# The first norm of a decoder block from tokens laid out by channels, with a product with ones in place of transposes

## The chip, the core and the metric

The kernel runs on one core of one Trainium2 chip. The metric is device time in microseconds (us); lower is better. Five engines work side by side, each through its own queue in a fixed order: TensorE (PE in the profile; PEld is its weight load), VectorE (DVE), ScalarE (ACT), GpSimd (POOL) and SyncE (SP), which here only issues DMAs. Every engine waits at the head of its own queue, so an instruction that waits holds up all that stand behind it on that engine.

## The reference

One decoder block over 2048 tokens of 1024 channels, in float32. What matters here is its beginning:

```
h    = x * rsqrt(mean(x*x, over channels) + 1e-6) * norm_pre_mix
proj = h @ w_in                       # 1024 -> 5376
q, k = rope(proj[:, :768]), rope(proj[:, 768:1536])
v    = proj[:, 1536:2304]             # 12 heads x 64
u, z, gate_a, gate_b = ...            # the remaining columns
```

Behind it follow dilated window attention, a gated branch, an output product, a second norm and an MLP. The norm's factor is one number per token, so it may stand ahead of a product with `h` or, for the rows that the product gives, behind it.

## The kernel before

Products in near-float32 accuracy are made of three: each operand is split into a high part (rounded to fp32r) and the rest, and `mm3` (lines 95 to 97) issues high by high, high by rest and rest by high. So every operand costs an ACT copy (high) and a DVE subtraction (rest).

The tokens are worked in four chunks `c` of 512 tokens, each of four blocks `i` of 128; block (0, 2) is the third of the first chunk. The tile `hT_a` holds a chunk of `h` with channels on the partitions, eight groups `k` of 128 channels, as high and rest. The program's start, up to about 87 us, runs `v_block` for the chunks 0 and 1: for a block, 24 matmuls 128x512 into the PSUM tile `va` (two of the three column groups of v), then 24 matmuls 128x256 into `vb`. In `v_block`, after the fourth of the eight `k` of `va`, a callback `between` puts the next block's `prenorm_cols` into PE's order. So the next block of `hT_a` has to be ready when the 12 remaining matmuls of `va` and the 24 of `vb` are done. Behind the v blocks come the q and k products of chunks 0 and 1 (`qk_pair`), and in the last of these pairs the four blocks of chunk 2 are normed; then v of chunks 2 and 3 (about 221 to 292 us), where `between` norms chunk 3.

Before the change a block's norm has two steps. `prenorm_rows` works with tokens on the partitions, one number per token: ACT squares with a running sum (line 204, two halves), DVE adds the halves and makes the reciprocal root in `rstd_of` (128x1 tensors, with one Newton step), and one DVE instruction scales the block in place (line 208). It is issued a block ahead. `prenorm_cols` then has PE transpose the eight 128x128 squares into two PSUM banks `pt` (line 219); ACT copies each bank into the high part (line 222), DVE subtracts for the rest (line 223), ACT copies once more into `hr` (line 245), which goes to memory (`hTd`). Block (0, 0) does the same with its gain broadcast through a product (`gpre`).

PE's order is the order in which the code is written. ACT, DVE, POOL and SP are ordered by a scheduler, except for the piece `as_written` at the start, which loads and splits the first v weights (`raw`, `wv`).

Of the kernel before, what the change touches and what calls it, by code (L numbers as in the profile page):

```python
# [41 lines left out]
def block_kernel(ctx, tc, a, out):  # L42
# [56 lines left out]
    def rstd_of(pl, ss, n, scale, tag):  # L99

        r = pl.tile([P, n], F32, name=f"r_{tag}", tag=f"rs_r{n}")
        act.activation(r, ss, AF.Sqrt, bias=eps, scale=scale)  # L102
        v = pl.tile([P, n], F32, name=f"v_{tag}", tag=f"rs_v{n}")
        dve.tensor_scalar(v, ss, scale, EPS, op0=OP.mult, op1=OP.add)
        dve.reciprocal(r, r)  # L105
        t = pl.tile([P, n], F32, name=f"t_{tag}", tag=f"rs_t{n}")
        if n == 1:
            dve.scalar_tensor_tensor(t, r, v, r, op0=OP.mult, op1=OP.mult)  # L108
        else:
            dve.tensor_mul(t, r, r)  # L110
            dve.tensor_mul(t, t, v)
        dve.tensor_scalar(t, t, -0.5, 1.5, op0=OP.mult, op1=OP.add)  # L112
        dve.tensor_mul(r, r, t)  # L113
        return r
# [60 lines left out]
    def behind():  # L175

        es, t = ExitStack(), mybir.EngineType
        for e in (t.Activation, t.DVE, t.Pool, t.SP):
            es.enter_context(tc.issue_after(next(i for i in reversed(nc.cur_bb.bb.instructions) if i.engine == e)))
        return es  # L180

    hT = {}
    xts = {}

    def cuts(c, i):

        n = 2 if (c, i) == (0, 0) else 1
        return [slice(h * D // n, (h + 1) * D // n) for h in range(n)]

    def load_x(c, i):  # L190
        xt = xp.tile([P, D], F32, name=f"x_{c}{i}", tag="x", bufs=4)
        for sl in cuts(c, i):
            sp.dma_start(xt[:, sl], x[c * 512 + i * P:c * 512 + (i + 1) * P, sl])
        xts[c, i] = xt

    def prenorm_rows(c, i, gs=None):

        if (c, i) not in xts:
            load_x(c, i)
        xt = xts[c, i]  # L200
        ss = sm.tile([P, 2], F32, name=f"ss_{c}{i}", tag="ss")
        for hf in range(2):
            junk = psum_aux(f"junk_{c}{i}{hf}")
            act.activation(junk, xt[:, hf * 512:(hf + 1) * 512], AF.Square, accum_out=ss[:, hf:hf + 1])
        dve.tensor_add(ss[:, 0:1], ss[:, 0:1], ss[:, 1:2])
        r = rstd_of(sm, ss[:, 0:1], 1, 1.0 / D, f"pre{c}{i}")
        for n, sl in enumerate(cuts(c, i)):
            dve.scalar_tensor_tensor(xt[:, sl], xt[:, sl], r, gs[n] if gs else gpre[:, sl], op0=OP.mult, op1=OP.mult)

    def prenorm_cols(c, i):  # L210

        if i == 0:
            hT[c] = hp.tile([P, 2, KT, 512], F32R, name=f"hT_a{c}", tag="hT", bufs=2)
        h, xt = hT[c], xts.pop((c, i))
        kept = []
        for k in range(0, KT, 4):
            pt = psum_aux(f"pt_{c}{i}{k}")
            for kk in range(4):
                pe.transpose(pt[:, kk * P:(kk + 1) * P], xt[:, (k + kk) * P:(k + kk + 1) * P], ident)
            hh, hl = (h[:, o, k:k + 4, i * P:(i + 1) * P] for o in range(2))  # L220
            p3 = pt.rearrange("p (k t) -> p k t", k=4)
            act.activation(hh, p3, AF.Copy)
            dve.tensor_sub(hl, p3, f32(hh))
            kept.append((k, p3))
            if (c, i) != (0, 0):
                keep_cols(c, i, kept)
        if i == 3:
            ks = slice(4 if c == 3 else 0, KT)
            if c != 2:
                for o in range(2):  # L230
                    sp.dma_start(hb_d[c][:, o, ks], f32(h)[:, o, ks])
        return kept

    hr2 = []

    def keep_cols(c, i, kept):
        while kept:
            k, p3 = kept.pop(0)
            if c == 2 and i % 2:
                if not k:  # L240
                    hr2.append(rp.tile([P, 2, 4, P], F32, name=f"hr_{c}{i}", tag="vt", bufs=2))
                raw = hr2[-1][:, k // 4]
            else:
                raw = xp.tile([P, 4, P], F32, name=f"hr_{c}{i}{k}", tag="hr", bufs=3)
            act.activation(raw, p3, AF.Copy)
            (sp if c < 2 else act).dma_start(hT_d[c, :, k:k + 4, i * P:(i + 1) * P], raw)
# [94 lines left out]
    def v_block(rp, wv, c, i, between=None):  # L341
# [13 lines left out]
        for o, n in ((pa, 2), (pb[:, :256], 1)):  # L355
# [4 lines left out]
            act.activation(hi, src, AF.Copy)  # L360
            dve.tensor_sub(lo, src, f32(hi))
# [3 lines left out]
    with ExitStack() as e1a:  # L365
        xp = stack(e1a, "xp", 2)
        pre = stack(e1a, "pre", 3)
        gpre = xp.tile([P, D], F32, name="gpre", bufs=1)
        rp = stack(e1a, "rp", 1, side="right")

        row = rp.tile([P, D], F32, name="row", tag="rope", bufs=2)
        busy = rp.tile([P, 256], F32, name="busy", tag="t1", bufs=2)
        pool.memset(row, 0.0)
        dve.memset(busy, 1.0)
        act.activation(warm, eps, AF.Sqrt)
        act.dma_start(row[0:1], a["norm_pre_mix"])
        act.dma_start(ident, a["ident"])
        p = psum_aux("busy")
        for _ in range(5):
            pe.matmul(p[:, :256], busy[:, :P], busy, start=True, stop=True)  # L380
        gp = [psum_mm(f"gpre{n}") for n in range(2)]
        for n in range(2):
            pe.matmul(gp[n], busy[:, :P], row[:, n * 512:(n + 1) * 512], start=True, stop=True)
        load_x(0, 0)
# [3 lines left out]
        wv = wide0, [third0[:, 0], third0[:, 1]]  # L388

        def early_load(g):  # L390
            for kk in range(2):
                sp.dma_start(raws[g][:, kk], w_src(6 + g, kk))

        def early(g, kk):
            w = part(wide0[kk], g) if g < 2 else third0[:, kk]
            return w[:, 0], w[:, 1], raws[g][:, kk]

        def hi(g, kk):
            w = early(g, kk)
            act.activation(w[0], w[2], AF.Copy)  # L400

        def lo(g, kk, eng):
            w = early(g, kk)
            eng.tensor_sub(w[1], w[2], f32(w[0]))

        with as_written():
            early_load(0)
            load_x(0, 1)
            early_load(1)
            early_load(2)  # L410
            prenorm_rows(0, 0, gp)
            p = psum_aux("busy")
            for _ in range(2):
                pe.matmul(p[:, :256], busy[:, :P], busy, start=True, stop=True)
            hi(0, 0)
            hi(0, 1)
            lo(0, 0, dve)
            kept = prenorm_cols(0, 0)
            lo(0, 1, dve)
            hi(1, 0)  # L420
            hi(1, 1)
            lo(1, 0, dve)
            lo(1, 1, dve)
            for n in range(2):
                act.activation(gpre[:, n * 512:(n + 1) * 512], gp[n], AF.Copy)
            prenorm_rows(0, 1)
            hi(2, 0)
            hi(2, 1)
            lo(2, 0, dve)
            lo(2, 1, dve)  # L430
            keep_cols(0, 0, kept)
# [52 lines left out]
        for half in range(2):  # L484
# [19 lines left out]
            for n, (g, which) in enumerate(qk):  # L504
# [9 lines left out]
                if not half and n == 5:  # L514
                    for i in range(4):
                        prenorm_rows(2, i)
# [1551 lines left out]
def _layout(inp):  # L2068
# [4 lines left out]
    d["norm_pre_mix"] = c(n["norm_pre_mix"])  # L2073
# [32 lines left out]
```

## Time and profile before

| | |
|---|---|
| median of 3 runs | 2643.76 us |
| lowest, highest | 2643.25, 2649.72 us |
| span of the profiled execution | 2646.3 us (no other time of that execution is given) |
| PE busy | 2614.2 us, 99% of the span |
| DVE, POOL, ACT busy | 63%, 45%, 41% |
| granted TensorE clock | 0.997 |
| PE waiting for transposes' input (line 219) | 2.6 us in 4 waits |

PE is busy nearly all the time, so the span is about PE's own work plus its waits. A time is to be read from PE's order: what PE no longer has to do comes off, and each wait that PE gets anew goes on, unless a wait further on shrinks by it.

### The profile page before, as it was taken

The page shows a single profiled execution, that of the slowest core. Times are in us where ns is not written, and L with a number is a line of the kernel's source. Part 1 is how long each engine was busy: PE and PEld are TensorE (multiplying, and loading weights), DVE is VectorE, ACT ScalarE, POOL GpSimd, SP SyncE. Part 2 cuts the span into 40 slices and gives each one's busy share as a digit, 9 for nine tenths or more (in the row PEclk, how much of TensorE's full clock was granted, in tenths as well). Part 3 has the DMA queues.
Part 4 walks back from the last instruction along what each step waited for, and adds up shares of the span by engine and source line. Part 5 has one row for each costly group of instructions (what it writes and reads, how often), then busy time and mean ns, then how long its engine had stood idle before and what let it go on. Part 6 is the DMA issues. An engine that isn't in the chain of part 4 may idle for free. (4 is left out here: it accounts for less than half of the span.)

```text
span 2646.3 us, 35496 instructions
## 1 busy us (share of the span) xinstructions
PE 2614.2 (99%) x12458; PEld 2184.1 (83%) x12458; DVE 1659.3 (63%) x2797; ACT 1092.9 (41%) x2286; POOL 1195.3 (45%) x1082
## 2 busy tenths in 40 slices
PE   9999999999999999999999999999999999999998
PEld 8888888788888877888877888888888888888886
DVE  5676665534443456765667664655438888888866
ACT  5213111254455344544446555655545333323334
POOL 0363354364454554211324572233225677666645
PEclk9999999999999999999999999999999999999999
DMA  8779778988898899744556464744443221222235
GB/s 321 286 243 330 258 233 286 299 278 257 290 292 227 231 292 348 261 140 167 213 194 252 155 219 143 230 124 124 123 136 108 88 85 60 88 88 88 88 117 210
DMA packets 389572, 527.25 MB, mean 199 GB/s; under 512 B 57041, under 2 KB 242129, under 8 KB 388370
## 3 DMA queue, kind: packets, MB, share of 16 engines
q1 hardware_dynamic: 300624, 434.98, 49.8%
q0 software_dynamic: 14992, 51.65, 5.1%
q10 hardware_dynamic: 73778, 38.35, 4.8%
q8 instruction: 98, 1.61, 0.2%
q14 instruction: 80, 0.66, 0.1%
HBM read 341.72 MB, written 183.17 MB: 198 GB/s over the span
## 5 line engine op out<-in xcount | busy, mean ns | idle before, releaser
L1957 PE MATMUL ya<-T_spots,s 128*128 128x512 f32 x1176 | 289.3, 389 | 0.7 <-ACT T_spots L70 0.5
L70 ACT ACTIVATE s<-sraw 128x768 fp32r<-128x768 f32 (+1 forms) x184 | 127.2, 696 | 330.4 <-POOL sraw L1758 155.7
L1957 PEld LDWEIGHTS ya<-T_spots,s 128*128 128x128 f32 x1176 | 220.5, 188 | 47.4 <-ACT T_spots L70 0.9
L78 DVE TENSOR_TENSOR s<-sraw,s 128x512 fp32r<-128x512 f32 x172 | 184.2, 1095 | 8.5 <-ACT s L70 5.9
L1428 PE MATMUL aa<-B,A 128*128 128x512 f32 x768 | 182.3, 390 | 1.5 <-ACT xs L1442 0.9
L1399 POOL TENSOR_TENSOR s<-w1r 128x512 f32<-128x512 f32 x32 | 42.4, 1324 | 306.7 <-DVE S L78 260.1
L724 PE MATMUL g<-opA,spots 128*128 128x512 f32 x672 | 170.8, 398 | 2.3 <-DVE cv L756 1.8
L1428 PEld LDWEIGHTS aa<-B,A 128*128 128x128 f32 x768 | 143.8, 188 | 32.1 <-ACT xs L1442 1.3
L724 PE MATMUL g<-opB,spots 128*128 128x512 f32 x648 | 164.0, 397 | 0.0
L1957 PE MATMUL yc<-T_spots,s 128*128 128x512 f32 x624 | 159.6, 389 | 0.0
L95 PE MATMUL x<-hT_a,wq 128*128 128x512 f32 x384 | 149.7, 390 | 0.0
L96 PE MATMUL x<-hT_a,wq 128*128 128x512 f32 x384 | 149.4, 389 | 0.0
L97 PE MATMUL x<-hT_a,wq 128*128 128x512 f32 x384 | 149.4, 389 | 0.0
L724 PEld LDWEIGHTS g<-opA,spots 128*128 128x128 f32 x672 | 120.9, 188 | 24.7 <-issue 2.2
L78 POOL TENSOR_TENSOR spots<-gr,spots 128x512 fp32r<-128x512 f32 x98 | 128.5, 1315 | 23.1 <-DMA gr<-in_w_in_dram 8.8
L1957 PEld LDWEIGHTS yc<-T_spots,s 128*128 128x128 f32 x624 | 117.1, 188 | 24.3
L724 PEld LDWEIGHTS g<-opB,spots 128*128 128x128 f32 x648 | 116.9, 188 | 21.2
L70 ACT ACTIVATE hl<-r 128x512 fp32r<-128x512 f32 x48 | 30.4, 633 | 236.5 <-POOL r L325 89.0
L974 DVE TENSOR_REDUCE o<-po 128x256 f32<-128x512 f32 x48 | 33.2, 691 | 133.1 <-PE po L973 133.1
L72 POOL TENSOR_SCALAR spots<-gr 128x512 fp32r<-128x512 f32 x86 | 55.4, 645 | 133.5 <-PE g L724 92.2
L1757 POOL TENSOR_TENSOR sraw<-sraw 128x256 f32<-128x256 f32 x56 | 41.9, 748 | 161.8 <-DVE s L78 158.8
L78 POOL TENSOR_TENSOR T_spots<-w2r,T_spots 128x512 fp32r<-128x512 f32 x70 | 104.4, 1519 | 7.3 <-ACT T_spots L70 7.3
(430 smaller groups left out, 6965.1 us busy)
## 6 DMA issues: line engine op xcount, KB each, us to landing
w1r<-in_w_mlp_in_dram SPq DMA_DIRECT2D x64, 512.0 KB, 3.7
sraw<-sd SPq DMA_DIRECT2D x128, 256.0 KB, 3.2
qk<-hl SPq DMA_DIRECT2D x24, 1024.0 KB, 5.6
qq<-qk SPq DMA_DIRECT2D x96, 256.0 KB, 5.2
w2r<-in_w_mlp_out_dram SPq DMA_DIRECT2D x16, 1024.0 KB, 7.9
sd<-u ACTq DMA_DIRECT2D x63, 256.0 KB, 3.7
g<-gated SPq DMA_DIRECT2D x56, 256.0 KB, 5.3
gr<-sgd SPq DMA_DIRECT2D x53, 256.0 KB, 4.5
```

Source lines behind the costliest of these rows:

```text
L70: act.activation(hi, src, AF.Copy)
L72: pool.tensor_scalar(hi, src, 1.0, 1.0, op0=OP.mult, op1=OP.mult)
L78: (pool if lo_eng == "pool" else dve).tensor_sub(lo, src, f32(hi))
L95: pe.matmul(ps, lh, rh, start=start, stop=False)
L96: pe.matmul(ps, lh, rl, start=False, stop=False)
L97: pe.matmul(ps, ll, rh, start=False, stop=stop)
L724: pe.matmul(p, w[:, l, k], h[:, r, k], start=i in (1, 6, 5, 4) and not k and not m, stop=k == 3 and m == 2, skip_group_check=True)
L974: dve.tensor_reduce(ot[:, :, j * 64:(j + 1) * 64], po.rearrange("p (b h e) -> p b e h", b=4, h=2), axis=AX.X, op=OP.add)
L1399: pool.tensor_add(s1, a21, a22)
L1428: pe.matmul(p, w[:, l, k, :], h[:, r, k, :], start=i in (1, 6, 5) and not k and not n, stop=k == 3 and n == 2, skip_group_check=True)
L1757: pool.tensor_add(a22, a21, a22)
L1957: pe.matmul(p, s[:, l], w[r], start=i in (1, 2, 5) and not m and not o, stop=m == 1 and o == 2, skip_group_check=True)
```

## The change

The host lays the tokens out a second time, as `x_cols`: for each block, channels on the partitions, 8x128 per partition. The gain comes as a 128x8 table (`gain`), one number per channel and thus per partition.

- A block's `x_cols` is loaded into `xb`. ACT squares it into `q` (two buffers), POOL adds the eight channel groups in three steps (512, 256, 128 elements), two blocks ahead (`squares`).
- `prenorm_cols` multiplies a matrix of ones by the 128x128 sums on PE: each partition of `pt` then holds every token's sum of squares. `rstd_of` now runs on 128x128 tensors, all partitions alike; DVE scales `xb` by gain and factor, one instruction for each channel group; ACT copies all 1024 elements to the high part, DVE subtracts for the rest. `xb` itself goes to memory, so the copies into `hr` are gone.
- Block (0, 0): `hT_a` is made from x times gain alone, without the norm's factor, and v's eviction multiplies by it (`first_r`). Its row layout is loaded too, for the sum of squares. Behind its v products, PE transposes the widened factor and DVE scales `xb` after the fact and makes `hT_a` anew for the q and k products. The loads and splits at the start are cut finer, in another order.

Core of the diff (moved comments and the unchanged parts of the start left out):

```diff
-    def rstd_of(pl, ss, n, scale, tag):
+    def rstd_of(pl, ss, n, scale, tag, bufs=2):
...
+    def squares(c, i):
+        if (c, i) not in xbs:
+            load_cols(c, i)
+        q = xp.tile([P, KT, P], F32, name=f"q_{c}{i}", tag="q", bufs=2)
+        act.activation(q, xbs[c, i], AF.Square)
+        for n in (4, 2, 1):
+            pool.tensor_add(q[:, :n], q[:, :n], q[:, n:2 * n])
+        qs[c, i] = q[:, 0]
...
     def prenorm_cols(c, i):
-        h, xt = hT[c], xts.pop((c, i))
-        for k in range(0, KT, 4):
-            pt = psum_aux(f"pt_{c}{i}{k}")
-            for kk in range(4):
-                pe.transpose(pt[:, kk * P:(kk + 1) * P], xt[:, (k + kk) * P:(k + kk + 1) * P], ident)
-            act.activation(hh, p3, AF.Copy)
-            dve.tensor_sub(hl, p3, f32(hh))
-            kept.append((k, p3))
-            if (c, i) != (0, 0):
-                keep_cols(c, i, kept)
+        (hh, hl), xb = cols_of(c, i), xbs.pop((c, i))
+        pt = psum_aux(f"pt_{c}{i}")[:, :P]
+        if (c, i) == (0, 0):
+            pe.transpose(pt, first_r, ident)
+            r = bass.AP(tensor=pt.tensor, offset=pt.offset, ap=[list(pt.ap[0]), [0, KT], [1, P]])
+            dve.tensor_tensor(xb, xb, r, op=OP.mult)
+        else:
+            pe.matmul(pt, ones, qs.pop((c, i)), start=True, stop=True)
+            r = rstd_of(xp, pt, P, 1.0 / D, f"pre{c}{i}", 1)
+            for k in range(KT):
+                dve.scalar_tensor_tensor(xb[:, k], xb[:, k], gain[:, k:k + 1], r, op0=OP.mult, op1=OP.mult)
+        act.activation(hh, xb, AF.Copy)
+        dve.tensor_sub(hl, xb, f32(hh))
+        (sp if c < 2 else act).dma_start(hT_d[c][:, :, i * P:(i + 1) * P], xb)
...
+            if (c, i) == (0, 0):
+                r = first_r[:, 0:1]
+                act.activation(hi, src, AF.Copy, scale=r)
+                dve.scalar_tensor_tensor(lo, src, r, f32(hi), op0=OP.mult, op1=OP.subtract)
...
+        with as_written():
+            load_cols(0, 0, halves[:1])
+            early_load(0, 0, FRONT)
+            early_load(0, 0, BACK)
+            load_cols(0, 0, halves[1:])
+            early_load(0, 1)
+            early_load(1, 0)
+            load_cols(0, 1)
+            early_load(1, 1)
+            xt = xp.tile([P, D], F32, name="x_00", tag="q", bufs=2)
+            sp.dma_start(xt, x[:P])
+            for kk in range(2):
+                early_load(2, kk)
...
+            act.activation(xt, xt, AF.Square, accum_out=ss)
+            r = rstd_of(sm, ss, 1, 1.0 / D, "pre00")
+            dve.tensor_copy(first_r, widen(r, P))
+            hi(2, 0)
+            lo(2, 0)
+            hi(2, 1)
+            lo(2, 1)
...
+                if n + 2 < len(mine) and not (half and mine[n + 2][0] == 2):
+                    squares(*mine[n + 2])
                 if nb and not (half and nb[0] == 2):
-                    if nb != (0, 1):
-                        prenorm_rows(*nb)
                     between = lambda nb=nb: prenorm_cols(*nb)
                 v_block(rp, wv, c, i, between)
+                if (c, i) == (0, 0):
+                    prenorm_cols(0, 0)
```

**DVE while v of block (0, 1) runs and block (0, 2) is prepared, before.** The first two rows are the subtractions behind the transposes; the rows after them belong to the block behind and to v's eviction (`vt`).

```order
L223 TENSOR_TENSOR hT_a_177<-pt_361,hT_a_177 128x4x128
L223 TENSOR_TENSOR hT_a_177<-pt_371,hT_a_177 128x4x128
L205 TENSOR_TENSOR ss_424<-ss_424 128x1
L104 TENSOR_SCALAR v_pre_432<-ss_424 128x1
L105 RECIPROCAL r_pre_430<-r_pre_430 128x1
L108 SCALAR_TENSOR_TENSOR t_pre_435<-r_pre_430,v_pre_432 128x1
```

The same place now:

```order
L104 TENSOR_SCALAR v_pre_338<-pt_334 128x128
L105 RECIPROCAL r_pre_336<-r_pre_336 128x128
L110 TENSOR_TENSOR t_pre_341<-r_pre_336 128x128
L111 TENSOR_TENSOR t_pre_341<-t_pre_341,v_pre_338 128x128
L112 TENSOR_SCALAR t_pre_341<-t_pre_341 128x128
L113 TENSOR_TENSOR r_pre_336<-r_pre_336,t_pre_341 128x128
L219 SCALAR_TENSOR_TENSOR xb_196<-xb_196,edge,r_pre_336 128x128 x8
L347 TENSOR_TENSOR vt_319<-va_320,vt_319 128x8x64
L221 TENSOR_TENSOR hT_a_154<-xb_196,hT_a_154 128x8x128
```

Between PE's product with ones (`pt_334`) and the rest of the high part (`hT_a`, last row) there now stand the whole root, 128 wide, and eight scalings; before, two subtractions stood there, and the root was made a block ahead.

**ACT at the same place, now.** `r_pre` is the square root; `q_400` is the square of the block two behind.

```order
L102 ACTIVATE r_pre_336<-pt_334,edge 128x128
L197 ACTIVATE q_400<-xb_398 128x1024
L346 ACTIVATE vt_319<-va_320 128x8x64
L220 ACTIVATE hT_a_154<-xb_196 128x8x128
L346 ACTIVATE vt_319<-vb_321 128x4x64
```

The square, behind which POOL's three additions start, stands directly behind the root of the block being prepared; its buffer comes free with that block's product with ones. The same pair stands in this order at blocks (0, 2), (0, 3), (1, 0), (3, 0) and (3, 1), and at (1, 3) the square stands beside the root too.

**DVE between v of block (0, 0) and v of block (0, 1), now.** `xb_140` is block (0, 0), `xb_147` block (0, 1), `pt_306` the transposed factor of block (0, 0).

```order
L214 TENSOR_TENSOR xb_140<-xb_140,pt_306 128x1024
L111 TENSOR_TENSOR t_pre_261<-t_pre_261,v_pre_258 128x128
L344 SCALAR_TENSOR_TENSOR vt_203<-vb_205,first_r,vt_203 128x4x64
L112 TENSOR_SCALAR t_pre_261<-t_pre_261 128x128
L113 TENSOR_TENSOR r_pre_256<-r_pre_256,t_pre_261 128x128
L221 TENSOR_TENSOR hT_a_154<-xb_140,hT_a_154 128x8x128
L219 SCALAR_TENSOR_TENSOR xb_147<-xb_147,edge,r_pre_256 128x128 x8
L221 TENSOR_TENSOR hT_a_154<-xb_147,hT_a_154 128x8x128
```

The second making of block (0, 0) (`xb_140`, first and sixth row) stands ahead of block (0, 1)'s scalings; its first row needs a PE transpose that PE issues behind all 72 v matmuls of block (0, 0).

**ACT while v of block (2, 0) runs, now.** `q_2114` is the square of block (3, 0), `hl_1964` belongs to the last q and k pair, `xb_1800` is block (2, 1).

```order
L346 ACTIVATE vt_1992<-va_1993 128x8x64
L197 ACTIVATE q_2114<-xb_2112 128x1024
L70 ACTIVATE hl_1964<-r_1977 128x512
L346 ACTIVATE vt_1992<-vb_1994 128x4x64
L220 ACTIVATE hT_a_1834<-xb_1800 128x8x128
```

The high part of block (2, 1), which v of that block needs first, stands behind the eviction of block (2, 0)'s `vb`, and so behind PE's last matmul for block (2, 0). Before, `hT_a` of all four blocks of chunk 2 stood ahead of v of block (2, 0).

More of the change, by code (lines that the diff above doesn't have):

```diff
@@ L210, in prenorm_cols @@
[L210 to L226 removed]
+            last = next((i for i in reversed(nc.cur_bb.bb.instructions) if i.engine == e), None)
@@ L230, in prenorm_cols @@
                 for o in range(2):
[L231 to L246, printed above, removed]
+                    sp.dma_start(hb_d[c][:, o, ks], f32(hT[c])[:, o, ks])
     def reload_h(c):
```

126 lines of the change are left out of this document (55 added, 71 removed).

## The prediction

> **What bounds the kernel now.** I read first who PE waited for, over the whole span, then the busy time of each engine block by block, then PE's own order of time in one block.
>
> ```profile
> PE pt L219 <- DVE x L208: 2.6, 4, 1.7
> 22.40:32.50 10.10, 9.56 (x60) 8.23 (x59) 6.72 (x19) 5.13 (x14) 0.00 (x0) 1.00 0.98 332
> 32.50:41.70 9.20, 9.20 (x58) 8.18 (x57) 4.48 (x12) 4.44 (x11) 0.00 (x0) 1.00 0.96 333
> 69.40:78.70 9.30, 9.30 (x59) 8.28 (x58) 4.58 (x13) 6.56 (x18) 0.00 (x0) 1.00 0.89 329
> 78.70:87.00 8.30, 8.30 (x50) 7.34 (x50) 8.12 (x18) 2.79 (x10) 3.03 (x2) 1.00 1.04 417
> ```
>
> The waits' columns are total, times and longest; 2.6 us is the largest of PE's waits. In the stretches (length, then busy PE, PEld, DVE, ACT, POOL, then clock, DMA share, GB/s) a v block takes 9.2 us and PE is busy for all of it; the last, with no norm behind it, takes 8.3. POOL does nothing there and DVE is half idle. So PE bounds this stage, and the rest has slack. PE inside a block:
>
> ```profile
> 35.24 1.03 PE L219 MATMUL pt<-ident,x 128*128 128x128 f32 x8
> 36.03 0.48 PE L95 MATMUL va<-wv,hT_a 128*128 128x512 f32 x1
> 36.35 0.40 PE L96 MATMUL va<-wv,hT_a 128*128 128x512 f32 x1
> 36.58 0.39 PE L97 MATMUL va<-wv,hT_a 128*128 128x512 f32 x1
> 38.85 0.28 PE L95 MATMUL vb<-wv,hT_a 128*128 128x256 f32 x1
> 41.72 0.40 PE L95 MATMUL va<-wv,hT_a 128*128 128x512 f32 x1
> ```
>
> Transposes hold PE from 35.24 to 36.03, and the matmul behind them comes 0.09 late: 0.9 us. A 512-wide matmul is 0.23 us apart from the next. From 36.03 to 41.72, 5.7 us, PE works on while the next block is prepared: that is the **cover**. Who needs how much of it:
>
> ```profile
> 35.88 1.09 ACT L222 ACTIVATE hT_a<-pt 128x512 fp32r<-128x512 f32 x2 [2.19 <-PE pt L219]
> 36.51 1.29 DVE L223 TENSOR_TENSOR hT_a<-pt,hT_a 128x512 fp32r<-128x512 f32 x2 [2.98 <-ACT hT_a L222]
> ```
>
> High and rest are done at 37.80, 2.6 us after the transposes began: 4 us to spare.
>
> **The chain that takes its place.** PE saves 0.9 us a block and gets one float32 product with ones, 128 wide. Matmul records in float32 come in twos there:
>
> ```profile
> L414 PE MATMUL busy<-busy 128*128 128x256 f32 x4 | 1.0, 379 | 0.0
> L380 PE MATMUL busy<-busy 128*128 128x256 f32 x10 | 4.2, 607 | 1.3 <-DVE busy L374 1.3
> ```
>
> Two 256-wide ones took 1.0 us, so I take 0.25 for 128 (half of 0.5). PE's own work falls by 0.65 us a block, 10 us over 15 blocks. But the root now lies between PE's product and the split, and everything in it is 128 wide. Its prices:
>
> ```profile
> L961 ACT ACTIVATE pf<-pT 128x128 f32<-128x128 f32 x20 | 5.2, 261 | 0.0
> L105 DVE RECIPROCAL r_pre<-r_pre 128x1 f32<-128x1 f32 x16 | 2.5, 158 | 4.9 <-ACT r_pre L102 4.9
> L997 DVE RECIPROCAL M<-M 128x16 f32<-128x16 f32 x4 | 1.0, 252 | 0.1
> L113 DVE TENSOR_TENSOR r_pre<-r_pre,t_pre 128x1 f32<-128x1 f32 x16 | 2.4, 154 | 0.2
> L458 DVE TENSOR_TENSOR ps<-ps 128x256 f32<-128x256 f32 x20 | 8.4, 418 | 8.9 <-DMA ps<-in_w_in_dram 8.9
> 473.57 1.11 DVE L546 SCALAR_TENSOR_TENSOR bsp<-rowsum,lngb,bsp 128x128 f32<-128x128 f32 x4
> L546 DVE SCALAR_TENSOR_TENSOR bsp<-rowsum,lngb,bsp 128x128 f32<-128x128 f32 x8 | 2.4, 335 | 0.0
> L404 DVE TENSOR_TENSOR wv<-raw,wv 128x1024 fp32r<-128x1024 f32 x6 | 7.2, 1220 | 0.0
> L400 ACT ACTIVATE wv<-raw 128x1024 fp32r<-128x1024 f32 x6 | 6.2, 1053 | 2.4 <-DMA raw<-in_w_in_dram 2.4
> ```
>
> A reciprocal grows from 158 ns for 1 element to 252 for 16: 6.3 ns each, where a product grows from 154 to 418 over 255, 1.0 ns each. So the reciprocal 128 wide is 0.158 + 127 x 0.0063 = 0.95 us, if the slope holds (bounds: 0.29 at a product's slope, 0.95 at its own; I take 0.93). The other four of the root are 0.154 + 0.13 = 0.29 each, with 0.04 between dependent ones. Four 128-wide scalings took 1.11 with 0.335 each, so 0.26 apart; eight take 7 x 0.26 + 0.335 = 2.15.
>
> From the start of the product with ones: 0.50 until its result is seen (0.25, and the 0.27 by which a transpose's record outlasts its place), root on ACT 0.27, reciprocal 0.97, four products 1.3, scalings 2.15, copy to the high part 1.1, subtraction 1.25: high at 6.3 and rest at 7.5 us. PE wants high after 0.25 + 5.6 = 5.85, and rest with its third matmul, at 6.3. So PE comes to the third matmul 1.2 late. From there to the next product with ones are ten matmuls, 2.28. **The period is 7.5 + 2.3 = 9.8 us against 9.2 before.** The gain on PE is eaten, and 0.6 is lost.
>
> **POOL on top.** It is idle there now, and gets three additions a block, two inputs each.
>
> ```profile
> L78 POOL TENSOR_TENSOR spots<-gr,spots 128x512 fp32r<-128x512 f32 x98 | 128.5, 1315 | 23.1 <-DMA gr<-in_w_in_dram 8.8
> L1757 POOL TENSOR_TENSOR sraw<-sraw 128x256 f32<-128x256 f32 x56 | 41.9, 748 | 161.8 <-DVE s L78 158.8
> L111 DVE TENSOR_TENSOR t_ln<-t_ln,v_ln x4: 161/162/1217, 505.2 to 1067.6; 128x4 f32<-128x4 f32 x4
> ```
>
> 1.3 + 0.75 + about 0.5 = 2.5 us. In the last row a four-element product took 162 ns in the middle and 1217 once: DVE was held for a time like a POOL instruction's. In the new order the square stands right behind the root at six of the ten blocks normed between v products, so its additions begin 1.9 us into the chain and meet its products and scalings. Bounds: 0 and 2.5 us a block; I take one hold by the longest, 1.3. The Trainium skill ("SBUF — State Buffer", section "SBUF: two separate sides") has VectorE and GpSimd share a port pair under an exclusive lock, held for a whole instruction; the 1217 agrees. By that rule all three additions hold DVE, which is my upper bound.
>
> **The start.** Weights arrive as fast as the DMA gives them:
>
> ```profile
> 8.38 1.06 ACT L400 ACTIVATE wv<-raw 128x1024 fp32r<-128x1024 f32 x1 [0.88 <-DMA raw<-in_w_in_dram]
> 12.53 1.06 ACT L400 ACTIVATE wv<-raw 128x1024 fp32r<-128x1024 f32 x1 [0.20 <-DMA raw<-in_w_in_dram]
> 9.97 0.39 PE L95 MATMUL va<-wv,hT_a 128*128 128x256 f32 x1 [0.90 <-ACT hT_a L222]
> 18.60 1.06 PE L219 MATMUL pt<-ident,x 128*128 128x128 f32 x8 [1.72 <-DVE x L208]
> 22.48 0.40 PE L95 MATMUL va<-wv,hT_a 128*128 128x512 f32 x1
> ```
>
> 1.5 MB had landed by 8.38 and 3 MB by 12.53: 1.4 us for 512 KB. PE's first v product can begin near 6.4 in place of 9.97, but soon waits for weights. The last third's halves are now the 8th and 9th 512 KB: 15.3 and 16.7. Copy and subtraction make the last ready near 19, and PE ends v of (0, 0) near 20.7 (before: 22.48). Then DVE alone, in its order: scaling of (0, 0) 1.25, product 0.33, `vt` 0.42, two 0.33, subtraction 1.22, eight scalings 2.15: 6.0 us, then the copy 1.1 and the subtraction 1.25. Block (0, 1) begins with 27.9, and its third matmul at 29.1 where it was 22.95: **+6**, and +8 if POOL, adding for the next two blocks just then, holds DVE. I take +7.
>
> **Chunk 2.** The pair's POOL work lies in the way of the additions:
>
> ```profile
> 209.43 1.03 PE L219 MATMUL pt<-ident,x 128*128 128x128 f32 x8
> 208.95 4.08 POOL L331 TENSOR_TENSOR r<-t,t 128x512 f32<-128x512 f32 x2 [4.14 <-DVE t L322]
> 258.61 1.09 PE L219 MATMUL pt<-ident,x 128*128 128x128 f32 x8 [0.17 <-DVE x L208]
> 277.51 1.09 PE L219 MATMUL pt<-ident,x 128*128 128x128 f32 x8 [0.17 <-DVE x L208]
> ```
>
> The transposes at 209.43 are block (2, 0)'s. Block (2, 2)'s sums are added behind POOL's work to 213 and two DMA issues, to about 216.7, while PE wants them at 209.43 + 2 x 3 = 215.4: 1.3. Block (2, 1)'s high part stands behind v of (2, 0) on ACT, so at least copy and subtraction, 2.3 - 0.45, are bare, and with DVE's four chains of 5.6 us among the q and k work up to 5. With 2.5 saved: +0.7 to +4; I take +3.
>
> **The sum.** Start +7. Blocks (0, 2) to (1, 3): six periods of 9.8 are 58.8 against 10.0 + 5 x 9.23 = 56.2, +2.6, and four holds of 1.3: +8. Chunk 2: +3. Chunk 3: the last two rows give 18.9 for two periods; four of 9.8 and two holds are 41.8 against 37.8: +4. In all **+22 us**, against a profiled span of 2646.3, which lies 2.5 above the median; no other time of that execution is shown. From the median: 2643.8 + 22 = **2666 us**. Bounds of the same mechanism: without holds, with the least of the start and of chunk 2, 6 + 2.6 + 0.7 + 1.4 = +11, and +7 if the reciprocal is a little cheaper; with holds of 2.5, 9 + 12.6 + 4 + 6.4 = +32. Nothing behind 292 us gives it back: PE is full there, and its later waits are small.
>
> **The rivals.** (1) *The chain is hidden and PE's saving shows.* 15 x 0.65 = 10 us and some 2 at the start: 2632. For it: the cover is 5.7 us and DVE was half idle. Against: with the reciprocal at 0.29 the rest is still ready at 6.85, a period of 9.15, even with before; it decides only below 6.3, so a second step of the chain would have to be cheaper by 0.5. (2) *A draw*: cheap reciprocal, no holds, the earlier start kept: 2643 to 2650. (3) *DMA comes in too.* ACT's square waits at its queue's head for the block's load, and the copy PE needs stands behind it. DMA is at 0.96 to 0.98 of its time there, but a buffer is free about 10 us ahead: 5 us at three blocks, 2681. (4) *PE's clock drops in the 7 us without work before block (0, 1)*: 607 ns for the first matmuls against 379 later show what that costs, 1.6 times, over some 4 us: +2, 2668. The Trainium skill ("TensorE: Matmul & The Clock Gate", Part 1) halves the clock after about 3.4 us idle; the granted clock reads 1.00 in the rows above, so this trace doesn't settle it.
>
> **Chances.** Forecast 0.72, with its own range 2651 to 2676; hidden 0.10; draw 0.09; DMA 0.05; clock 0.04. About 0.3%, 8 us, is what a measurement can tell here. The draw and a tenth of the forecast lie within that: same 0.16; faster 0.10; slower 0.74. The range leaves out the hidden case and the far end of DMA: 2645 to 2685.
>
> **What would show it.** Right: PE waits for `hT_a` (ACT line 220, DVE line 221) at nearly each v block, 1 to 3 us each; the 128-wide reciprocal near 0.9 us; block (0, 1) starting near 28; q and k starting near 102 in place of 87. Wrong: a v block of 8.6 us with no wait, a reciprocal near 0.3, or scalings that don't lengthen beside POOL's additions.

## The result, and the profile after

| | before | changed |
|---|---|---|
| median of 5 runs | 2643.76 us | 2700.85 us |
| lowest, highest | 2643.25, 2649.72 | 2696.45, 2703.79 |
| ratio | | 1.0213, 95% interval 1.0201 to 1.0226 |
| span of the profiled execution | 2646.3 | 2698.8 |
| PE busy | 2614.2, 99% | 2623.3, 97% |
| granted TensorE clock | 0.997 | 0.989 |

The change makes the kernel 57 us slower. Forecast were 22, with a range up to 2685. By marks in PE's order of time (the transposes or the product with ones of a block, the first matmuls of a stage) the 52.5 us between the two spans fall into five pieces:

| piece | before | changed | difference | forecast |
|---|---|---|---|---|
| start, to block (0, 2)'s transposes or product with ones | 25.93 | 33.89 | +8.0 | +7 |
| from there to the first q and k product | 61.07 | 80.86 | +19.8 | +8 |
| q and k of chunks 0 and 1, v of chunk 2 up to block (3, 0)'s mark in (2, 3) | 162.04 | 179.52 | +17.5 | +3 |
| what is left of v of (2, 3), and of chunk 3 | 43.39 | 52.41 | +9.0 | +4 |
| all the rest | 2353.9 | 2352.1 | -1.8 | 0 |

PE's waits by what ended them, over the whole span of the changed kernel (total, times, longest):

```profile
PE va L95 <- ACT hT_a L220: 36.7, 13, 8.3
PE va L97 <- DVE hT_a L221: 5.5, 11, 0.5
PE pt L216 <- POOL q L199: 1.9, 1, 1.9
```

PE now waits at 13 blocks for the high part and at most of them right behind it for the rest. That is 44 us with the wait for POOL's sums, and 2.6 us of waits for the transposes' input are gone. The stretches show what else there is. The columns are the length, then busy PE, PEld, DVE, ACT, POOL, then clock, DMA share, GB/s; first the last 6.3 of the 8.3 us in which PE waits ahead of block (0, 1), then the periods behind the products of (0, 3) and (1, 1), then chunk 2 and chunk 3.

```profile
22.48:28.80 6.32, 0.00 (x0) 0.00 (x0) 5.16 (x14) 1.46 (x2) 1.64 (x3) 0.53 0.59 207
47.40:60.88 13.48, 10.73 (x51) 8.73 (x50) 8.26 (x17) 3.24 (x5) 2.49 (x3) 0.87 0.48 187
74.36:84.60 10.24, 9.16 (x51) 7.59 (x50) 6.60 (x17) 2.29 (x4) 0.00 (x0) 1.00 0.31 104
248.35:294.27 45.92, 33.56 (x159) 27.21 (x158) 39.74 (x77) 10.94 (x17) 15.98 (x16) 0.85 0.68 231
294.27:346.68 52.41, 45.01 (x238) 37.40 (x236) 36.75 (x79) 11.68 (x19) 9.52 (x12) 0.93 0.62 225
```

The same two stages before:

```profile
221.20:249.04 27.84, 27.84 (x159) 24.43 (x158) 15.98 (x29) 7.46 (x18) 8.64 (x9) 1.00 1.06 368
249.04:292.43 43.39, 43.04 (x262) 37.85 (x260) 23.26 (x50) 17.95 (x42) 5.22 (x7) 1.00 0.75 274
```

There are two kinds of v block: 10.2 us with POOL at rest and the clock at 1.00, and 13.5 us with 2.5 us of POOL and the clock at 0.87. (The period behind the product of (1, 2) lies between them: 11.3 us, 4.9 us of POOL, clock 1.00.) In chunk 2 DVE is busy for 39.7 of 45.9 us, where it was busy for 16.0 of 27.8. The chain in the two kinds of block, on DVE and POOL (additions beside it in the first six rows, none in the others):

```profile
48.43 0.94 DVE L105 RECIPROCAL r_pre<-r_pre 128x128 f32<-128x128 f32 x1
49.21 2.65 POOL L199 TENSOR_TENSOR q<-q 128x512 f32<-128x512 f32 x3 [9.62 <-ACT q L197]
49.41 1.24 DVE L110 TENSOR_TENSOR t_pre<-r_pre 128x128 f32<-128x128 f32 x1
50.69 0.78 DVE L111 TENSOR_TENSOR t_pre<-t_pre,v_pre 128x128 f32<-128x128 f32 x1
51.50 0.44 DVE L112 TENSOR_SCALAR t_pre<-t_pre 128x128 f32<-128x128 f32 x1
52.30 2.19 DVE L219 SCALAR_TENSOR_TENSOR xb<-xb,edge,r_pre 128x128 f32<-128x128 f32 x8
...
75.39 0.94 DVE L105 RECIPROCAL r_pre<-r_pre 128x128 f32<-128x128 f32 x1
76.37 0.29 DVE L110 TENSOR_TENSOR t_pre<-r_pre 128x128 f32<-128x128 f32 x1
76.69 0.29 DVE L111 TENSOR_TENSOR t_pre<-t_pre,v_pre 128x128 f32<-128x128 f32 x1
77.02 0.23 DVE L112 TENSOR_SCALAR t_pre<-t_pre 128x128 f32<-128x128 f32 x1
77.61 2.19 DVE L219 SCALAR_TENSOR_TENSOR xb<-xb,edge,r_pre 128x128 f32<-128x128 f32 x8
80.92 1.23 DVE L221 TENSOR_TENSOR hT_a<-xb,hT_a 128x1024 fp32r<-128x1024 f32 x1 [0.52 <-ACT hT_a L220]
```

The reciprocal takes 0.94 us, the additions stretch the three steps behind it from 0.81 to 2.46, so the chain is 7.84 us long without them and 9.5 with them. And PE, in the same two places:

```profile
55.64 0.51 PE L95 MATMUL va<-wv,hT_a 128*128 128x512 f32 x1 [2.23 <-ACT hT_a L220]
56.90 0.70 PE L97 MATMUL va<-wv,hT_a 128*128 128x512 f32 x1 [0.53 <-DVE hT_a L221]
...
80.94 0.50 PE L95 MATMUL va<-wv,hT_a 128*128 128x512 f32 x1 [0.56 <-ACT hT_a L220]
82.20 0.50 PE L97 MATMUL va<-wv,hT_a 128*128 128x512 f32 x1 [0.53 <-DVE hT_a L221]
82.53 0.39 PE L95 MATMUL va<-wv,hT_a 128*128 128x512 f32 x1
31.09 0.63 PE L96 MATMUL va<-wv,hT_a 128*128 128x512 f32 x1
31.51 0.63 PE L97 MATMUL va<-wv,hT_a 128*128 128x512 f32 x1
```

Behind the wait of 0.6 a matmul takes 0.39 us and the next stands 0.23 behind it. Behind the long wait ahead of (0, 1) they take 0.63 and stand 0.42 apart, for some 4 us; the eight rows from 56.90 to 59.95 read alike. Up to the end of chunk 3, 71 of `mm3`'s matmuls of 512 columns last over 0.52 us, and none in the kernel before. At 0.42 to 0.43 apart in place of 0.23, some of them only in part, each loses about 0.195: I estimate 71 x 0.195 = 13.8 us of slow clock, 1.8 at the start, 5.8 in chunks 0 and 1, 3.5 in chunk 2, 2.7 in chunk 3.

### The profile page after: what moved, and what is told of

It is laid out like the page before. It is cut to its first block, busy times and chain, and to the rows that moved or that the text cites. A ratio compares the mean times of both kernels' runs of the same rounds, so it can differ in the third digit from the quotient of the medians.

```text
span 2698.8 us, 35283 instructions
## 1 busy us (share of the span) xinstructions
PE 2623.3 (97%) x12357; PEld 2184.3 (81%) x12357; DVE 1714.8 (64%) x2890; ACT 1074.6 (40%) x2192; POOL 1230.8 (46%) x1127
```

## The experiments

The theory now: the chain is longer than PE's cover, POOL's additions lengthen it further, a wait of 2.2 us and more lowers PE's clock behind it, and in chunk 2 DVE has more work than time. Each is tried apart. "Above" is the distance of the median from that of the kernel before on the same chip (2639.5 to 2641.1 us there); the changed kernel stands at +57. Most intervals reach about 4 us to each side, so that a difference of 5 us between two rows says little by itself; the stretches say more.

| run | median | ratio | interval | above |
|---|---|---|---|---|
| without the additions | 2670.5 | 1.0115 | 1.0100 to 1.0130 | +31 |
| squares late | 2678.2 | 1.0144 | 1.0129 to 1.0159 | +39 |
| PE filled | 2690.3 | 1.0185 | 1.0168 to 1.0201 | +51 |
| PE filled less | 2689.9 | 1.0183 | 1.0168 to 1.0198 | +49 |
| without Newton's step | 2666.1 | 1.0098 | 1.0081 to 1.0115 | +27 |
| product early | 2673.0 | 1.0116 | 1.0099 to 1.0133 | +32 |
| chunk 2 without scaling | 2681.5 | 1.0162 | 1.0145 to 1.0179 | +41 |
| chunk 2 early | 2693.1 | 1.0199 | 1.0184 to 1.0214 | +52 |
| chunk 2 earlier still | 2699.0 | 1.0220 | 1.0205 to 1.0235 | +59 |
| all together | 2703.3 | 1.0233 | 1.0218 to 1.0248 | +63 |
| all together, reordered | 2659.9 | 1.0077 | 1.0060 to 1.0094 | +20 |
| mixed | 2647.6 | 1.0022 | 1.0012 to 1.0032 | +7 |

**The additions left out.**

```diff
-        for n in (4, 2, 1):
+        for n in ():
             pool.tensor_add(q[:, :n], q[:, :n], q[:, n:2 * n])
```

> Leaves out POOL's three additions per block (the sums of squares are then those of the first channel group alone, so the norm's factor is another number; all else runs). Mine (chain 7.84 us long, lengthened where POOL adds, and PE's granted clock falling where the wait grows to 2.7 us): the v blocks of 13.5 us become 10.2 like the one that no addition touches, no matmul of 512 stays at 0.63 us except behind the long wait at the start. 3.25 x 3 + 1.0 + 3 in chunks 0 and 1, about 6 in chunk 3, 1.5 at the start, up to 6 in chunk 2: -27, about 2674. Rival A (the slow clock has another cause than the waits): only the held time goes, about 1.7 x 6 + 1 + 7: 2682. Rival B (the additions hold nobody, the chain's own length is all): no change, 2701.

26 us went, as forecast (27). A v block and chunk 2 of this run:

```profile
42.66:52.92 10.26, 9.17 (x51) 7.58 (x50) 6.61 (x17) 3.25 (x5) 0.00 (x0) 1.00 0.62 225
230.99:273.16 42.17, 33.02 (x160) 27.27 (x159) 34.89 (x76) 10.77 (x17) 10.65 (x10) 0.88 0.78 267
```

All six blocks of chunks 0 and 1 take 10.3 us at full clock, and the first q and k product comes at 99.6 in place of 114.75: 15 us. But chunk 2 still takes 42.2 us. So the additions explain the difference between the two kinds of block, and little of chunk 2.

**The additions moved.** ACT squares behind v's last eviction, so that the additions run while DVE has nothing to do.

```diff
-                if n + 2 < len(mine) and not (half and mine[n + 2][0] == 2):
-                    squares(*mine[n + 2])
+                late = n + 2 < len(mine) and not (half and mine[n + 2][0] == 2)
...
                 v_block(rp, wv, c, i, between)
+                if late:
+                    with behind():
+                        squares(*mine[n + 2])
```

> All work stays. The square of the block two behind, and with it POOL's additions, stands on ACT behind the eviction of v's last third in place of behind the root, in chunks 0, 1 and 3: the additions fall into the 2.9 us in which DVE has nothing to do. Mine: the v blocks fall from 13.5 to about 10.2, as without additions; chunk 2 and the start stay: -18, about 2683, and the granted clock is 1.00 between 50 and 100 us. Rival (the additions slow the chain wherever they stand, through the delay of the sums): 2701 or more.

18 us went, as forecast. The additions take the same 2.5 us and DVE's busy time per block is that without them (6.61):

```profile
44.83:55.44 10.61, 9.41 (x51) 7.51 (x51) 6.61 (x17) 3.24 (x5) 2.48 (x3) 1.00 0.56 207
```

So it is their place beside the chain that costs, not the work.

**PE filled, to keep its clock.** Products of ones with ones stand ahead of a block's `va`, where PE would wait; `FILL` holds their number for each block.

```diff
-        pb = psum_mm(f"vb_{c}{i}")
+        pb = psum_mm(f"vb_{c}{i}"); pf = psum_aux(f"fill_{c}{i}") if FILL.get((c, i)) else None; [pe.matmul(pf[:, :P], ones, ones, start=True, stop=True) for _ in range(FILL.get((c, i), 0))]
```

> All work stays; PE gets products of ones with ones, 128 wide (0.14 us each), in the time in which it waits: 46 ahead of block (0, 1), 14 ahead of each block with the 2.2 us wait, 28 and 38 ahead of (2, 0) and (2, 1). Mine (a wait of about 2.7 us lowers PE's clock for some 4 us after it): the matmuls behind keep 0.39 us, 1.6 us less in each of six blocks, 2.3 at block (0, 1), about 4 in chunk 2: -16, about 2685, although PE does more. Rival (the slow matmuls come from something else that these blocks share, the evictions or POOL): 2701 or some us above it, and matmuls at 0.63 us in the same places.

> As the run with PE filled, but with fewer products: one of ones with ones took 0.22 us there (14 took 3.13), so now 36 ahead of (0, 1), 10 ahead of the blocks with the 2.2 us wait, 21 and 27 ahead of (2, 0) and (2, 1), 9 ahead of (3, 0) and (3, 1), none ahead of (1, 2). Mine (wait lowers the clock): the filled blocks keep a period of 11.9 (9.5 of chain with additions and 2.4 of matmuls at full clock) in place of 13.5, 1.6 x 6, 2.2 at the start, 4 to 5 in chunk 2: 15 to 16 below the changed kernel. Rival (PE's extra products cost what the clock gives): 5 below, as in the first such run.

The first filled more than the waits: 14 products hold PE for 3.05 us, ahead of waits of 2.2. It won 6 us, not 16. In the second a filled block reads so:

```profile
44.20:56.12 11.92, 11.39 (x71) 9.84 (x70) 8.27 (x17) 3.25 (x5) 2.49 (x3) 1.00 0.54 193
50.06 2.40 PE L325 MATMUL fill<-ones_p 128*128 128x128 f32 x20
```

The period is 11.9, the clock 1.00, and no matmul behind the fill is longer than 0.50: exactly the 1.6 us that were forecast, in a block with the same chain and the same additions. So it is PE's wait that lowers the clock. The total is 8 us below the changed kernel (12 by the spans), not 15: chunk 2 gave 2.3 in place of 4 to 5, since its second block still waited 2.8 behind the fill, and the block behind (1, 2), left unfilled, waited 2.8 in place of 2.1. That block kept its full clock this time; the last section shows what decides.

**A shorter chain.** Square root and reciprocal alone.

```diff
-            r = rstd_of(xp, pt, P, 1.0 / D, f"pre{c}{i}", 1)
+            r = xp.tile([P, P], F32, name=f"r_pre{c}{i}", tag="rs_r128", bufs=1); act.activation(r, pt, AF.Sqrt, bias=eps, scale=1.0 / D); dve.reciprocal(r, r)
```

> The root of the blocks behind the first is square root and reciprocal alone: the 128-wide scaling of the sum and the four steps of Newton's correction (L104, L110 to L113) are left out, so the factor is a little less exact. The chain is 1.45 us shorter, 6.4 us, about what PE's cover allows. DVE and ACT are ordered anew by this: block (0, 1) comes ahead of the second making of block (0, 0), and the squares of (0, 2) stand elsewhere. Mine: blocks without additions in their chain take 8.5 us without a wait, those with additions 10.4 without the slow clock: -18 in chunks 0 and 1, -8 in chunk 3, -3 at the start, -4 to -8 in chunk 2: about 2666. Rival (no link between wait and clock): 1.45 in each of 13 blocks and 3 at the start, 2679. Rival (the holds alone matter): 2695 or more.

30 us went, against 35 forecast. Blocks without additions in the chain take 8.8 us with no wait, those with them 10.7 at full clock, but one in chunk 3 takes 12.3 with a slow stretch; chunk 2 falls to 35.6. A chain 1.45 us shorter is worth about twice that in a block, since the clock stays up as well.

**A longer cover.** The product with ones stands nine matmuls earlier.

```diff
-                if between and k == 3:
+                if between and k == 0:
```

> One number: the product with ones stands behind the first channel group of va in place of the fourth, nine matmuls (2.1 us) earlier, so PE's cover grows from 6.3 to 8.4 us for the rest. Mine: blocks without additions in the chain (7.84) take 8.5 without a wait, those with additions (9.5) take 9.8 with a wait of some 1.3 and full clock: -19 in chunks 0 and 1, -10 in chunk 3, chunk 2 and the start stay: 29 below the changed kernel. Rival (DVE as a whole is the limit of a block: its evictions and the chain do not fit the period): blocks of 10 still, 15 to 20 below.

25 us went, against 29. A block with additions in the chain, then one without:

```profile
51.23:61.07 9.84, 9.13 (x51) 7.58 (x50) 8.26 (x17) 3.26 (x5) 2.49 (x3) 1.00 1.01 427
61.07:69.66 8.59, 8.59 (x52) 7.61 (x51) 6.35 (x17) 2.30 (x4) 0.00 (x0) 1.00 0.83 300
```

Both are as forecast (9.8 and 8.5). The second is what the saving on PE is worth where nothing waits: 8.6 against 9.2 before.

**Chunk 2.** First, DVE's work is taken away there: no root and no scaling for its four blocks.

```diff
-            r = rstd_of(xp, pt, P, 1.0 / D, f"pre{c}{i}", 1)
-            for k in range(KT):
+            r = rstd_of(xp, pt, P, 1.0 / D, f"pre{c}{i}", 1) if c != 2 else None
+            for k in range(KT if c != 2 else 0):
```

> For chunk 2 alone the root and the eight scalings are left out (its tokens go on as they are, without norm and gain), products with ones and POOL's additions stay but nobody waits for them. Mine (DVE's amount of work is the bound there): v of chunk 2 starts without the wait of 4.9 and runs at 28 to 30 us: 16 to 18 below the changed kernel. Rival (the queue on POOL and ACT behind the rope, not DVE's own work): 5 below or less.

```profile
252.75:281.42 28.67, 28.25 (x159) 24.67 (x158) 15.95 (x22) 4.95 (x9) 15.96 (x16) 1.00 0.79 286
```

Chunk 2 takes 28.7 us and DVE is busy for 15.95, as before the change (27.84 and 15.98). POOL does as much as in the changed kernel. So DVE's root and scaling cost the 17 us. By the times 16 went, as forecast, and 21 by the spans: 17.3 in chunk 2, less 4.4 ahead of it, where a product with ones waits 4.2 for POOL's sums, and 8 behind chunk 3, where the two kernels are alike. That last stretch reads 2344 to 2354 us in the traces of all these kernels, so 8 us there say nothing.

Then the same work was only moved forward: product, root and scaling of one block in each of four pairs ahead, first in the second to fifth pair, then in the first to fourth.

```diff
+                if not half and 0 < n < 5:
+                    squares(2, n - 1)
+                    between = lambda i, n=n: i == 3 and scale_cols(2, n - 1)
                 if not half and n == 5:
-                    for i in range(4):
-                        squares(2, i)
                     between = lambda i: prenorm_cols(2, i)
```

> Of chunk 2 alone the product with ones, the root and the scaling are done earlier, one block in each of four q and k pairs ahead, in place in xb; high and rest of hT_a are made where they were. All work stays. Mine (chunk 2's chains stand in DVE's order behind the rope of the last pairs, and again behind the splits of v's weights): the waits of 4.9, 6.6 and 1.9 us there and the slow clock behind them go: 18 below the changed kernel, and DVE and POOL have room for it in the q and k pairs. Rival (DVE and POOL are too full at the end of the q and k stage, so that the copies and subtractions come late all the same): 5 below or less.

> As the run with chunk 2's products, roots and scalings ahead, but each one q and k pair earlier still (the first to the fourth pair in place of the second to the fifth), so that none is left in the 50 us before v of chunk 2. Mine (DVE has more to do there than there is time for, about 12 us of scalings and roots and 7 of holds on top of 31 in 50): chunk 2 falls from 46 to about 29 us, 16 to 18 below the changed kernel. Rival (DVE and POOL are short of time over the whole q and k stage, and every delay is handed on): again 5 below.

Here I was wrong twice: 4 us and none. v of chunk 2 took 41.5 and 41.3 us all the same. PE's waits from 120 to 360 us in the second run, and POOL ahead of the weights' copies:

```profile
PE vb L95 <- POOL wv L72: 8.7, 1, 8.7
PE x L95 <- DVE t L311: 6.0, 2, 3.2
261.92 3.86 POOL L199 TENSOR_TENSOR q<-q 128x512 f32<-128x512 f32 x3 [3.05 <-ACT q L197]
268.79 2.05 POOL L72 TENSOR_SCALAR wv<-wv_r 128x1024 fp32r<-128x1024 f32 x2
```

PE waits no longer for chunk 2's norm but for the weights of v's last third, which POOL copies and DVE splits, and for PSUM banks that DVE's rope products free late. Ahead of the copies POOL has the additions of two blocks of chunk 3 in its queue (at 261.92 and 266.23). They wait for squares, which wait on ACT for their blocks' loads (1.5 and 3.3 us), so the copies come at 268.79, where the kernel before made them at 220.67, with its last q and k product. In the first of these runs one such row of additions stands ahead, and PE waits 3.9 us for the same copies. So with DVE's work moved away the order in POOL's queue kept chunk 2 long, and DVE's share in it is only argued: how much is left with the copies ahead of the additions wasn't tried.

**All changes that helped, together.** Product early, squares late, chunk 2 ahead, block (0, 0) made anew behind (0, 1), and the gain moved to ACT, so that one DVE product replaces eight scalings:

```diff
             for k in range(KT):
-                dve.scalar_tensor_tensor(xb[:, k], xb[:, k], gain[:, k:k + 1], r, op0=OP.mult, op1=OP.mult)
+                act.activation(xb[:, k], xb[:, k], AF.Copy, scale=gain[:, k:k + 1])
+            dve.tensor_tensor(xb, xb, bass.AP(tensor=r.tensor, offset=r.offset, ap=[list(r.ap[0]), [0, KT], [1, P]]), op=OP.mult)
```

> Together: the product with ones three channel groups earlier; squares behind v's evictions; the gain multiplied on ACT beside the root (eight scalings 128x128) and one DVE product with the root's row in place of eight DVE scalings; block (0, 0) made anew behind block (0, 1); chunk 2's products, roots and scalings in the q and k pairs ahead. All work stays. Mine: v blocks of 8.5 us without a wait in chunks 0, 1 and 3, chunk 2 without a wait; the start still 2 to 4 us later than before the change: 0 to 6 us below the kernel before. Rival (ACT's eight scalings and the additions still lengthen the chain): 10 to 20 above the kernel before.

```profile
PE pt L219 <- POOL q L199: 31.8, 9, 4.1
```

Two of the edits met: the square stood at the end of one block and the product at the start of the next, so PE waited 3.4 us a block for POOL's sums, 31.8 in all, and the kernel ended at +63 where 0 to 6 below the kernel before were forecast. With the squares three blocks ahead, and chunk 2 in the first to fourth pair:

> As the run with all changes together, mended where its trace showed PE waiting 3.4 us a block for POOL's sums (the square stood at the end of one block, the product at the start of the next): squares three blocks ahead, and chunk 2's products and roots in the first to fourth q and k pair. Mine: v blocks of 8.5 to 9, chunk 2 at about 29, start of (0, 1) near 24.5: between 4 us below and 8 above the kernel before. Rival (three additions a block hold DVE, which is full now, by over 1 us in each block): 12 to 20 above the kernel before.

```profile
47.26:55.84 8.58, 8.58 (x52) 7.61 (x50) 5.80 (x10) 4.90 (x14) 2.50 (x3) 1.00 1.06 441
228.79:267.92 39.13, 27.89 (x148) 24.25 (x148) 26.81 (x33) 10.66 (x22) 16.34 (x15) 0.87 0.90 318
```

v blocks take 8.6 us now with the additions inside, though two in chunks 0 and 1 stay at 10.1 and 10.5, one of them with a wait of 1.8 for POOL's sums. Chunk 3 takes 42.5 against 43.4 before. Chunk 2 remains at 39 (PE waits 9.4 us for a split of v's last third: POOL's copies are done at 236.25, DVE comes to the split at 243.27), and q and k begin 6 us later than before. It ends at +20, where I had forecast 4 below to 8 above; the rival said 12 to 20 above.

**Mixed.** The kernel before, with the new norm only where the experiments had shown room: (0, 2) to (1, 3) and chunk 3.

> Built on the kernel before: blocks (0, 0), (0, 1) and chunk 2 keep their row norm and transposes; (0, 2) to (1, 3) and chunk 3, ten blocks, are normed from x laid out by channels, with the product with ones behind the first channel group of va, the square one block ahead of it, the gain on ACT, one DVE product with the root's row. Mine (a v block with nothing in PE's way took 8.44 us in the run with the early product, 9.23 before): 10 x 0.79 less, up to 2 of it given back where POOL's additions hold DVE: 6 to 8 below the kernel before. Rival (smaller buffers for x and for the raw copies, and 1.2 us more of DVE and 2 of ACT a block, bring the waits back elsewhere): 0 to 10 above.

It is 7 us slower than the kernel before (6 by the ratio, with an interval of 3 to 8), so my forecast fell and the rival held. The v blocks take 8.7 to 8.9, but for one of 10.6 that waits 1.9 for POOL's sums, and q and k begin at 86.4 against 87.0, although block (0, 1) began 0.3 later. Chunk 2 gives it back, with the old norm: its PE waits, from 0 to 300 us,

```profile
PE pt L251 <- ACT hr L277: 3.3, 2, 2.8
PE vb L96 <- DVE wv L78: 2.8, 2, 1.5
```

name the raw copies `hr`, for which this kernel had two buffers in place of three to make room for `q`, and DVE's splits. That the third buffer would cure it wasn't tried. No version that I ran beats the kernel before.

## Why the prediction failed, point by point

**The direction and the mechanism held.** PE does wait at nearly every v block, for the high part (ACT line 220) and then the rest (DVE line 221). Making the chain shorter, the cover longer, or the additions disappear each took 25 to 30 us off.

**The start: +7 taken, +8.0 measured.** PE ended v of (0, 0) at 20.3 (20.7 forecast) and began block (0, 1) at 28.8 (27.9), behind the work of DVE that was named.

**The chain: 7.5 forecast, 7.84 measured; the period 9.8 forecast, 10.24 measured.** The reciprocal (0.93 taken, 0.94 measured), the products (0.29) and the scalings (2.15 and 2.19) were right. Missing was 0.26 ahead of the reciprocal: the root's square root took 0.37 on ACT, and the scaling of the sum (line 104) stands ahead of the reciprocal. The ten matmuls took 2.40, not 2.28. Six blocks: 2.6 us.

**The holds: 1.3 a block taken, 1.0 to 1.8 measured, at five of six blocks in place of four.** 7.9 us in place of 5.2, by what the chain and the clock leave of the 19.8. The bounds of 0 and 2.5 held. The Trainium skill ("SBUF — State Buffer", section "SBUF: two separate sides") lets the instruction that starts first keep the shared port pair to its end. The trace agrees in that the three DVE steps shown above each end 0.08 to 0.15 us behind one of POOL's three additions. Of their 2.65 us, 1.65 hold DVE there, about two thirds, since one DVE step gets through at each addition.

**The step that failed: the clock, priced once.** Rival (4) put the loss of clock only behind the 7 us ahead of block (0, 1), +2 in all, and the sum put it at nothing behind the v blocks' waits of 1.2, and 1.3 more from a hold, without giving a reason. It said that the trace before doesn't settle what a wait does to the clock, and went by rows of the first 87 us. Further on that trace has just such a pair of waits, with the slow matmuls behind it:

```profile
1021.07 0.50 PE L95 MATMUL z<-w_z,hT_b 128*128 128x512 f32 x1 [1.90 <-DMA hT_b<-hbd]
1022.37 0.79 PE L97 MATMUL z<-w_z,hT_b 128*128 128x512 f32 x1 [0.56 <-DMA hT_b<-hbd]
1022.96 0.63 PE L95 MATMUL z<-w_z,hT_b 128*128 128x512 f32 x1
```

So the price of a wait of about 2.5 us could have been read beforehand. The start's part of the clock came as priced (1.8 us). But the waits of 2.2 us, with 0.5 more right behind, lowered the clock at six of the seven blocks with additions: 5.8 us in chunks 0 and 1, 6.2 in chunks 2 and 3. Of the 19.8 us in chunks 0 and 1, 6.1 are the chain, 7.9 the holds, 5.8 the clock.

**And the term that was mis-sized: chunk 2, +3 taken with +0.7 and +4 as bounds, +17.5 measured.** I let DVE's four chains stand "among the q and k work" at a cost of up to 5 and never summed DVE's time there. Block (2, 0)'s chain shows it:

```profile
243.96 0.28 DVE L104 TENSOR_SCALAR v_pre<-pt 128x128 f32<-128x128 f32 x1
248.90 3.62 DVE L219 SCALAR_TENSOR_TENSOR xb<-xb,edge,r_pre 128x128 f32<-128x128 f32 x8
253.65 1.22 DVE L221 TENSOR_TENSOR hT_a<-xb,hT_a 128x1024 fp32r<-128x1024 f32 x1 [1.12 <-ACT hT_a L220]
255.39 4.14 DVE L78 TENSOR_TENSOR wv<-wv_r,wv 128x1024 fp32r<-128x1024 f32 x2
265.06 5.10 DVE L219 SCALAR_TENSOR_TENSOR xb<-xb,edge,r_pre 128x128 f32<-128x128 f32 x8
```

Its product with ones had run at 237.18. DVE came to it at 243.96, took 11 us with rope and additions in between, and then split v's weights ahead of block (2, 1), whose scalings took 5.1. "Half idle" was true of DVE over the v blocks and not here, and holds by POOL made its work longer than the sum of its instructions: eight scalings take 2.19 us alone, and here 3.62 beside POOL's copies of weights and 5.10 beside its additions.

**Chunk 3: +4 taken, +9.0 measured.** Two of four blocks had additions and the slow clock, 13.0 and 13.3 us against a forecast of 9.8 and one hold each.

**The rivals.** The hidden chain, the draw and the DMA rival didn't come in the changed kernel (the last shows only in the runs with chunk 2 ahead, where squares wait for their loads): with the product early the chain is hidden in a block without additions, which shows that the cover was the point, as rival (1) had it. The range ended at 2685 because the clock and chunk 2 were both left at their small values; the far end of the forecast's own bounds (+32, with 9 for a start that had been bounded by 8) lacked both.

## What to carry to other kernels

An edit that takes work off the engine that bounds a stage is priced by the chain that it puts between that engine's output and its next input: time saved on PE is worth nothing until that chain fits the cover, here 7.8 us against 6.3. A wait that recurs has to be priced with all that follows from it, each time, and work moved to an engine that is idle on average has to be summed with what that engine does in the very stage where it lands, holds included. Where the chain's head depends on nothing late, it should be issued earlier before anything else is tuned.

## What the hardware showed that I had not expected

- PE's clock fell behind waits far shorter than 7 us. Of 25 places, over the changed kernel and four experiments, where PE waited 2.2 to 2.4 us for the high part and mostly 0.5 more for the rest, 22 were followed by 6 to 9 slow matmuls, starting up to 2.3 us behind the wait's end and lasting 3 to 4 us. Two waits of 0.6 and 0.5 never were, 1.6 and 0.5 not in the changed kernel; one of 1.0 and 0.5 in the run without Newton's step was, and three like it there were not. So length alone doesn't decide; where the wait lies in time does. In each of the 14 traces all changes of the granted clock lie whole multiples of 3.413 us apart (in the changed kernel at 43.38, 46.79, 57.03, 60.44, 70.68 and so on). Cut at these times, PE's busy time in one stretch tells the clock of the next. Four stretches of the changed kernel, two and two in a row (length, busy PE and the rest as above, then clock):

```profile
39.96:43.37 3.41, 0.73 (x2) 0.30 (x2) 2.89 (x8) 1.33 (x2) 0.00 (x0) 1.00 0.35 106
43.37:46.79 3.42, 3.33 (x8) 2.65 (x9) 0.37 (x2) 0.00 (x0) 0.00 (x0) 0.50 0.83 286
91.16:94.57 3.41, 1.84 (x7) 1.23 (x8) 2.06 (x3) 2.21 (x3) 2.13 (x3) 1.00 0.53 159
94.57:97.98 3.41, 3.41 (x18) 2.82 (x17) 1.26 (x3) 1.43 (x2) 1.49 (x4) 1.00 0.98 347
```

  Over the 14 traces, of all stretches at full clock in which PE was busy for less than 45% the next one had half the clock (82 of 82), of those with 45 to 55% 13 of 32, and of those with more none (of 10586; 8 to 2650 us). So a wait lowers the clock where it takes more than about half of one such stretch, and a wait that lies across two may not: the three of the 25 that kept the clock left PE busy for 0.48 and 0.72, 0.50 and 0.70, and 0.64 and 0.55 of two stretches. That it hit three blocks in a row was helped by the period: 13.5 us is close to four stretches, 13.65. The Trainium skill ("TensorE: Matmul & The Clock Gate", Part 1) puts the drop behind about 3.4 us of idle, watched in windows that run free of the kernel. The trace agrees with such windows, and not with a wholly idle one: 1.9 us of idle in 3.4 were always enough.
- Three additions of POOL, 2.65 us in all, made three dependent DVE steps of 128 elements 1.65 us longer, the longest from 0.29 to 1.24, and eight scalings from 2.18 to 3.93 in another block.
- Products of ones with ones, 128 wide in float32, took 0.22 us each in a row of 10 or 14; a single one between v's matmuls moved the next by 0.14, and the one behind that by 0.08 more.
